# The second layer's scan: one 128-wide product for two heads, or one 64-wide product for each

## The chip, the cores and the metric

The kernel runs on one core of a Trainium2 chip. The metric is the device time of one execution in microseconds (us), as the median of three runs; a run without a profile and the profiled execution differ by well under a tenth of a per cent here.

## The reference

A decoder trunk of two residual layers over 512 tokens and a width of 2048, all in float32. The first is gated differential attention. The second, which the change is in, is RWKV-7 time mixing: `p = h @ w_in` gives r, k, v, a gate and two low-rank inputs, each mixed with the token before, and then every one of 32 heads of 64 channels runs a recurrence over the tokens with a 64 x 64 state S:

```
def step(S, inp):
    r_t, w_t, k_t, v_t, a_t, b_t = inp
    sa = einsum('bhvk,bhk->bhv', S, a_t)
    S = S * w_t[:, :, None, :] + sa[..., None] * b_t[:, :, None, :] + v_t[..., None] * k_t[:, :, None, :]
    y = einsum('bhvk,bhk->bhv', S, r_t)
    return S, y
```

with `a = -kk` and `b = kk * iclr` (kk is the normalised key). The y of a head is normalised, weighted, gated and projected: `x + (y * silu(g)) @ w_out`.

## The kernel before

The recurrence is not stepped token by token. Tokens are cut into 8 chunks of 64 (`NC_ = 8`, `C = 64`), and a chunk becomes a few small matrix products. Two heads are handled together as a pair (j = 0 to 15): head 0 lies on partitions 0 to 63 and head 1 on 64 to 127 (`HEADS`, slices `r_`).

`scan_pair` is the serial part. For each chunk c it makes three products that depend on one another, into one PSUM tile `sm`:

1. line 1558: `sm <- VS,G`. `VS[:, c]` holds, for each head, the state on the head's own 64 partitions and the chunk's values on the other 64. `G` holds the matching matrix, so state and values are summed over 128 partitions in one product.
2. line 1569: `sm <- rhs,TT`, the product with the triangular inverse of the chunk. `rhs` is product 1 copied out by ScalarE (line 1561, once for each head). `TT` is 128 x 128 with the two heads' 64 x 64 matrices on its diagonal and zeros beside them.
3. line 1576: `sm <- VS,BKT`, the state's increment. ScalarE has copied product 2 into `VS` (line 1571), and VectorE then decays and adds (line 1580, in chunk 0 line 1583) into the `VS` of the next chunk.

Of products 1 and 3 both heads are computed against both heads' columns, 128 x 128 outputs, of which the two diagonal blocks are read. GpSimd copies the states aside (`SA`, line 1564) and prepares the decayed state (`Sg`, line 1567). The last chunk has no product 3. In all there are 16 x 8 products 1, as many products 2, and 16 x 7 products 3: 368.

These chains run between the big projections. All weights are split into a high and a low part (`split_w`: ScalarE casts at line 105, VectorE subtracts at line 106), and `mm3` (line 124) makes three 512-wide products of each weight block. Every one of them calls `tick`, which counts down; when the gap that `scan_pair` has yielded is used up, the next step of the chain is issued right there in TensorE's program. So the three products of a step stand 4 to 8 big products apart. When a chain has done its chunks, `outputs` (lines 1598 and 1602) makes the reads of all chunks, in one burst: line 1598 takes a 128 x 64 stationary block and 64 columns, line 1602 a 64 x 64 block and 64 columns. `t_combine` (lines 1465 and 1476, 32 x 32 blocks) and `gram` (lines 1344 and 1361) make other small products, also in bursts.

In the profile a float32 product counts as two records of TensorE, each with its weight load (PEld); the big ones (float32r) count as one. "128*64" in a record is the part of the array it uses, rows by columns.

Of the kernel before, what the change touches and what calls it, by code (L numbers as in the profile page):

```python
# [23 lines left out]
P = 128  # L24
# [1167 lines left out]
C = 64  # L1192
# [342 lines left out]
HEADS = ((0, slice(0, C)), (1, slice(C, P)))  # L1535


def chain(g, j, p, delay, gap, gap_s, others=(), lead=GAP_D - GAP_T):
    def steps():
        yield from t_combine(g, j, p, lead)  # L1540
        yield from scan_pair(g, j, p, gap, gap_s, dict(others))

    p.chain = Chain(g, steps(), delay)
    return p.chain


def scan_pair(g, j, p, gap, gap_s, others):

    nc, w, VS = g.nc, g.work, p.VS
    both = lambda ap: ap.rearrange("p h n -> p (h n)")
    p.SA = w.tile([P, NC_ - 1, C], F32, name="SA", tag="SA", bufs=1)
    for h, r_ in HEADS:
        g.begun = nc.gpsimd.memset(VS[r_, 0, h, :], 0.0).ins
    for c in range(NC_):
        sm = g.ps.tile([P, 512], F32, name="sm", tag="pa", bufs=1)
        nc.tensor.matmul(sm[:, 0:P], both(p.G[:, c, 0]), both(VS[:, c]), start=True, stop=True)  # L1558
        rhs = w.tile([P, C], F32, name="rhs", tag="rhs", bufs=2)
        for h, r_ in HEADS:  # L1560
            nc.scalar.copy(rhs[r_, :], sm[r_, h * C : h * C + C])  # L1561
        if c:
            for h, r_ in HEADS:
                nc.gpsimd.tensor_copy(p.SA[r_, c - 1, :], VS[r_, c, h, :])  # L1564
        if 0 < c < NC_ - 1:
            Sg = w.tile([P, C], F32, name="Sg", tag="Sg", bufs=2)
            nc.gpsimd.tensor_scalar(Sg[:], p.SA[:, c - 1, :], p.gam[:, c : c + 1], None, ALU.mult)
        yield gap
        nc.tensor.matmul(sm[:, P : P + C], both(g.TT[j % 2][:, c]), rhs[:], start=True, stop=True)  # L1569
        for h, r_ in HEADS:  # L1570
            g.copied = nc.scalar.copy(VS[r_, c, h, :], sm[r_, P : P + C])  # L1571
        yield gap
        if c == NC_ - 1:
            break
        o = P + C
        nc.tensor.matmul(sm[:, o : o + P], p.BKT[:, c, :], both(VS[:, c]), start=True, stop=True)  # L1576
        for h, r_ in HEADS:
            s_ = sm[r_, o + h * C : o + h * C + C]
            if c:
                g.state = nc.vector.scalar_tensor_tensor(VS[r_, c + 1, h, :], s_, p.gam[r_, c : c + 1], Sg[r_, :],  # L1580
                                                         ALU.mult, ALU.add)
            else:
                nc.vector.tensor_scalar(VS[r_, c + 1, h, :], s_, p.gam[r_, c : c + 1], None, ALU.mult)
        if c in others:
            others[c]()
        yield gap_s
    outputs(g, j, p)
    centre(g, p)


def outputs(g, j, p):

    nc = g.nc
    p.Y = [g.ps.tile([P, 512], F32, name="Y", tag="pc", bufs=2) for _ in range(2)]
    place = lambda h, c: p.Y[h][c % 2 * C : c % 2 * C + C, c // 2 * C : c // 2 * C + C]
    for c in range(NC_):
        for h, _ in HEADS:
            nc.tensor.matmul(place(h, c), p.G[:, c, 1, h, :], p.VS[:, c, h, :], start=c < 2, stop=c == 0,  # L1598
                             skip_group_check=True)
    for c in range(1, NC_):  # L1600
        for h, r_ in HEADS:
            nc.tensor.matmul(place(h, c), p.AR[r_, c, 1, :], p.SA[r_, c - 1, :], start=False, stop=True,
                             skip_group_check=True)


def centre(g, p):

    nc, w, Y = g.nc, g.work, p.Y
    s1 = g.small.tile([P, NT, 2], F32, name="s1", tag="s1", bufs=3)
    p.yc = w.tile([P, 2 * NT, C], F32, name="yc", tag="yc", bufs=1)  # L1610
    for h in range(2):
        yg = Y[h][:, : NT * C].rearrange("p (t n) -> p t n", t=NT)
        nc.vector.reduce_sum(s1[:, :, h], yg, AX.X)
        nc.vector.tensor_scalar(s1[:, :, h], s1[:, :, h], 1.0 / C, None, ALU.mult)
        c = nc.vector.tensor_sub(p.yc[:, h::2, :], yg, s1[:, :, h : h + 1].to_broadcast([P, NT, C]))
    g.centred = c.ins
# [255 lines left out]
```

## Time and profile before

| | |
|---|---|
| median of 3 runs | 2055.09 us (2055.05 to 2055.22) |
| profiled execution | 2055.6 us, of which 2053.9 us from first to last instruction |
| TensorE (PE) busy | 2035.2 us, 99% |
| weight loads (PEld) busy | 1673.1 us, 81% |
| VectorE (DVE) busy | 1605.9 us, 78% |
| ScalarE (ACT) busy | 1133.6 us, 55% |
| GpSimd (POOL) busy | 400.3 us, 19% |
| clock granted to TensorE | 1.000 of full speed |

TensorE is busy nearly all the time, and the other engines run beside it. A row of the timeline reads: start, duration, engine, line, operation, output<-inputs, part of the array, shapes, count. The ends of matmuls are modelled and overlap the next one, so what a product takes of TensorE is read from starts: from the start of one to the start of the next. The scan of the 16 pairs lies between about 1008 and 1910 us.

### The profile page before, as it was taken

The numbers are of one execution on the slowest core, as the hardware profiler recorded it, in microseconds if no ns is written. First come the engines' busy times: TensorE is split into PE (matmuls) and PEld (weight loads), VectorE is DVE, ScalarE is ACT, GpSimd is POOL, SyncE is SP. The second block draws the span as 40 slices with busy tenths as digits, with TensorE's granted clock in tenths as the row PEclk, the third lists the DMA queues.
The fourth block names the chain that finished last, engine by engine and source line by source line (L and its number), as shares of the span: only waits on it lengthen the run. The fifth ranks groups of instructions, "written<-read, shape, count | busy, mean of one in ns | idle before, by whom it ended". The sixth has DMA issues, their size and how long they took to land.

```text
span 2053.9 us, 34174 instructions
## 1 busy us (share of the span) xinstructions
PE 2035.2 (99%) x11922; PEld 1673.1 (81%) x11922; DVE 1605.9 (78%) x4100; ACT 1133.6 (55%) x2258; POOL 400.3 (19%) x782
## 2 busy tenths in 40 slices
PE   9999999999999999999999999999999999999999
PEld 7888888888888888888877778888888888877887
DVE  7988988888898977476787888787777888777745
ACT  5765656666666544355565555555555555545423
POOL 1020111102011000121222222322222222231011
PEclk9999999999999999999999999999999999999999
DMA  8487978879787965823333323223333232346676
GB/s 288 156 163 192 182 172 186 164 192 167 190 180 171 274 218 172 175 87 108 103 83 92 94 77 98 92 89 98 98 98 98 87 96 83 111 127 201 212 182 145
DMA packets 159534, 297.76 MB, mean 145 GB/s; under 512 B 64529, under 2 KB 81937, under 8 KB 159361
## 3 DMA queue, kind: packets, MB, share of 16 engines
q1 hardware_dynamic: 110768, 184.39, 28.8%
q0 software_dynamic: 25952, 90.88, 23.2%
q10 hardware_dynamic: 22640, 20.30, 3.1%
q8 instruction: 94, 1.54, 0.3%
q14 instruction: 80, 0.65, 0.1%
HBM read 271.33 MB, written 24.18 MB: 144 GB/s over the span
## 4 chain that ended last, share of the span: by engine, by line
PE 90%; DVE 6%; ACT 2%; issue 1%; DMA 1%; SPq 0%; ACTq 0%; DVEq 0%
PE pp L124 45%; PE pp L574 24%; PE pt L124 5%; PE gp L1361 2%; DVE wl L106 2%; PE sm L1558 1%; PE sc L124 1%; PE o L124 1%; PE sm L1576 1%; PE sm L1569 1%; ACT wh L105 1%; PE Y L1598 1%; PE pt L296 1%; PE z L124 1%; PE pt L1393 1%
## 5 line engine op out<-in xcount | busy, mean ns | idle before, releaser
L106 DVE TENSOR_TENSOR wl<-wraw,wh 128x1024 fp32r<-128x1024 f32 (+1 forms) x286 | 349.7, 1223 | 167.7 <-ACT wh L105 157.0
L105 ACT CAST wh<-wraw 128x1024 fp32r<-128x1024 f32 (+1 forms) x286 | 299.5, 1047 | 237.6 <-PE pp L124 115.8
L124 PE MATMUL pp<-hL,wh 128*128 128x512 f32 x1024 | 413.6, 404 | 0.0
L124 PE MATMUL pp<-hH,wl 128*128 128x512 f32 x1024 | 413.0, 403 | 0.0
L124 PE MATMUL pp<-hH,wh 128*128 128x512 f32 x1024 | 412.3, 403 | 0.2 <-ACT wh L105 0.2
L124 PEld LDWEIGHTS pp<-hH,wh 128*128 128x128 f32 x1024 | 193.1, 189 | 34.5 <-ACT wh L105 0.4
L124 PEld LDWEIGHTS pp<-hL,wh 128*128 128x128 f32 x1024 | 193.1, 189 | 33.5
L124 PEld LDWEIGHTS pp<-hH,wl 128*128 128x128 f32 x1024 | 193.2, 189 | 32.4
L574 PE MATMUL pp<-wh,hH 128*128 128x512 f32 x448 | 176.8, 395 | 0.0
L574 PE MATMUL pp<-wh,hL 128*128 128x512 f32 x448 | 175.8, 392 | 0.0
L124 PE MATMUL pp<-wh,hH 128*128 128x512 f32 x376 | 147.0, 392 | 0.6 <-ACT hH L1147 0.6
L124 PE MATMUL pp<-wl,hH 128*128 128x512 f32 x376 | 147.5, 392 | 0.0
L124 PE MATMUL pp<-wh,hL 128*128 128x512 f32 x376 | 147.3, 392 | 0.1
L1420 DVE SCALAR_TENSOR_TENSOR tmpl<-LT,Tm 128x60 f32<-128x60 f32 (+24 forms) x496 | 134.8, 272 | 13.2
L574 PE MATMUL pp<-wl,hH 128*128 128x512 f32 x448 | 140.3, 392 | 0.0
L1564 POOL COPY SA<-VS 64x64 f32<-64x64 f32 x224 | 55.4, 248 | 397.8 <-DVE VS L1580 375.4
L1422 DVE TENSOR_TENSOR Tm<-Tm,tmpl 128x60 f32<-128x60 f32 (+24 forms) x496 | 103.4, 209 | 11.7
L1561 ACT COPY rhs<-sm 64x64 f32<-64x64 f32 x256 | 53.0, 207 | 84.8 <-PE sm L1558 81.8
L574 PEld LDWEIGHTS pp<-wl,hH 128*128 128x128 f32 x448 | 84.5, 189 | 17.2
L574 PEld LDWEIGHTS pp<-wh,hH 128*128 128x128 f32 x448 | 84.2, 188 | 17.5 <-issue 0.4
L574 PEld LDWEIGHTS pp<-wh,hL 128*128 128x128 f32 x448 | 84.3, 188 | 16.1
L1571 ACT COPY VS<-sm 64x64 f32<-64x64 f32 x256 | 52.9, 207 | 76.2 <-PE sm L1569 70.3
(435 smaller groups left out, 4374.4 us busy)
## 6 DMA issues: line engine op xcount, KB each, us to landing
wraw<-in_rw_w_in_dram SPq DMA_DIRECT2D x128, 512.0 KB
wraw<-in_da_w_in_dram SPq DMA_DIRECT2D x75, 512.0 KB
wraw<-in_da_w_in_dram POOLq DMA_DIRECT2D x28, 512.0 KB, 6.6
wraw<-in_da_w_out_dram SPq DMA_DIRECT2D x26, 512.0 KB
wraw<-in_rw_w_out_dram SPq DMA_DIRECT2D x24, 512.0 KB
Ta<-in_da_w_in_dram POOLq DMA_DIRECT2D x21, 512.0 KB, 5.6
Tb<-in_da_w_in_dram POOLq DMA_DIRECT2D x21, 512.0 KB, 5.7
Tc<-in_da_w_in_dram POOLq DMA_DIRECT2D x21, 512.0 KB, 5.5
```

Of the source, the lines that this page charges most:

```text
L105: a = nc.scalar.copy(hi[:, ks], raw[:, ks])
L106: d = nc.vector.tensor_sub(lo[:, ks], raw[:, ks], hi[:, ks].bitcast(F32))
L124: m = nc.tensor.matmul(out, a, b, start=s, stop=e, skip_group_check=skip)
L296: nc.tensor.transpose(pt[:, c * P : (c + 1) * P], t1s[t][:, c * P : (c + 1) * P], g.ident[:])
L574: m = nc.tensor.matmul(out[t][:], x, wt[lo][:, k, :], start=first, stop=end and lo == 1 and k == KG - 1, skip_group_check=True)
L1361: m = nc.tensor.matmul(gp[h][:, i * P : (i + 1) * P], BK[r_, c0 + i, :, :], p.AR[r_, c0 + i, :, :], start=True, stop=True)
L1393: nc.tensor.transpose(ps[:, i * P : (i + 1) * P], p.BK[:, c0 + i].rearrange("p s t -> p (s t)"), g.ident[:])
L1420: nc.vector.scalar_tensor_tensor(tt, LT[:, i : i + 1, i + 1 :].to_broadcast([P, s, n]), n2[:, i : i + 1], Tm[:, 0:s, i : i + 1].to_broadca ...
L1422: nc.vector.tensor_add(Tm[:, 0:s, i + 1 :], Tm[:, 0:s, i + 1 :], tt)
L1561: nc.scalar.copy(rhs[r_, :], sm[r_, h * C : h * C + C])
L1564: nc.gpsimd.tensor_copy(p.SA[r_, c - 1, :], VS[r_, c, h, :])
L1571: g.copied = nc.scalar.copy(VS[r_, c, h, :], sm[r_, P : P + C])
```

## The change

Each of the three products is issued once for each head, with the head's 64 output columns alone. Product 1 and 3 take 128 x 64 of stationary block and 64 moving columns for each head; product 2 takes the head's 64 x 64 block of `TT` and 64 columns. A head's result now lies on its own partitions, in the same 64 columns of `sm`, so `rhs` is filled by one copy of 128 partitions instead of two of 64. The copies into `VS` and the VectorE updates stay one for each head.

```
-        nc.tensor.matmul(sm[:, 0:P], both(p.G[:, c, 0]), both(VS[:, c]), start=True, stop=True)
+        for h, r_ in HEADS:
+            nc.tensor.matmul(sm[r_, 0:C], p.G[:, c, 0, h, :], VS[:, c, h, :], start=True, stop=True)
         rhs = w.tile([P, C], F32, name="rhs", tag="rhs", bufs=2)
-        for h, r_ in HEADS:
-            nc.scalar.copy(rhs[r_, :], sm[r_, h * C : h * C + C])
+        nc.scalar.copy(rhs[:], sm[:, 0:C])
...
         yield gap
-        nc.tensor.matmul(sm[:, P : P + C], both(g.TT[j % 2][:, c]), rhs[:], start=True, stop=True)
         for h, r_ in HEADS:
-            g.copied = nc.scalar.copy(VS[r_, c, h, :], sm[r_, P : P + C])
+            nc.tensor.matmul(sm[r_, C:P], g.TT[j % 2][r_, c, h, :], rhs[r_, :], start=True, stop=True)
+        for h, r_ in HEADS:
+            g.copied = nc.scalar.copy(VS[r_, c, h, :], sm[r_, C:P])
...
-        o = P + C
-        nc.tensor.matmul(sm[:, o : o + P], p.BKT[:, c, :], both(VS[:, c]), start=True, stop=True)
         for h, r_ in HEADS:
-            s_ = sm[r_, o + h * C : o + h * C + C]
+            nc.tensor.matmul(sm[r_, P : P + C], p.BKT[:, c, r_], VS[:, c, h, :], start=True, stop=True)
+        for h, r_ in HEADS:
+            s_ = sm[r_, P : P + C]
```

On TensorE, in the scan of a late pair, products 1 and 2 of a chunk (G and TT are the matrices of the chunk) stand so before:

```order
L124 MATMUL pp<-hL,wh 128x512
L1558 MATMUL sm<-VS,G_12808 128x128
L124 MATMUL pp<-hH,wl 128x512
L124 MATMUL pp<-hH,wh 128x512
L124 MATMUL pp<-hL,wh 128x512
L124 MATMUL pp<-hH,wl 128x512
L124 MATMUL pp<-hH,wh 128x512
L124 MATMUL pp<-hL,wh 128x512
L1569 MATMUL sm<-rhs,TT_9497 128x64
```

and after:

```order
L124 MATMUL pp<-hL,wh 128x512
L1558 MATMUL sm<-VS,G_12868 64x64 x2
L124 MATMUL pp<-hH,wl 128x512
L124 MATMUL pp<-hH,wh 128x512
L124 MATMUL pp<-hL,wh 128x512
L124 MATMUL pp<-hH,wl 128x512
L124 MATMUL pp<-hH,wh 128x512
L124 MATMUL pp<-hL,wh 128x512
L1569 MATMUL sm<-rhs,TT_9497 64x64 x2
```

The two heads' products stand side by side, the big products around them are where they were, and the gap is the same. So it is with nearly all of the 368. On ScalarE, in the same scan, the copies out of product 1 and what stands behind them were:

```order
L1394 COPY BKT<-pt 128x512
L1561 COPY rhs<-sm 64x64 x2
L105 CAST wh<-wraw 128x1024
L1187 ACTIVATE mixv<-pp,omu 128x512
L1571 COPY VS<-sm 64x64 x2
```

and are:

```order
L1394 COPY BKT<-pt 128x512
L1560 COPY rhs<-sm 128x64
L105 CAST wh<-wraw 128x1024
L1187 ACTIVATE mixv<-pp,omu 128x512
L1571 COPY VS<-sm 64x64 x2
```

One copy stands where two stood; here nothing else has moved.

More of the change, by code (lines that the diff above doesn't have):

```diff
@@ L1551, in scan_pair @@
     nc, w, VS = g.nc, g.work, p.VS
-    both = lambda ap: ap.rearrange("p h n -> p (h n)")
     p.SA = w.tile([P, NC_ - 1, C], F32, name="SA", tag="SA", bufs=1)
```

## The prediction

> **What bounds the kernel now.** I read the page's busy shares and the chain that ended last first, then the time by stage, then the groups of the three products, and last the timeline of single products, since the groups give durations and not what a product takes of TensorE.
>
> ```profile
> span 2053.9 us, 34174 instructions
> PE 2035.2 (99%) x11922; PEld 1673.1 (81%) x11922; DVE 1605.9 (78%) x4100; ACT 1133.6 (55%) x2258; POOL 400.3 (19%) x782
> PE 90%; DVE 6%; ACT 2%; issue 1%; DMA 1%; SPq 0%; ACTq 0%; DVEq 0%
> ```
>
> ```profile
> 1008.00:1910.00 902.00, 893.17 (x6463) 729.56 (x6462) 704.81 (x1955) 499.41 (x1160) 244.15 (x581) 1.00 0.35 102
> ```
>
> The second fence is the stage of the scan: its length, then busy time of PE, PEld, DVE, ACT and POOL, then the granted clock (1.00). TensorE stands idle 902.0 - 893.2 = 8.8 us of it. VectorE has 197 us to spare and ScalarE 403 us. So in this stage time is TensorE time: what a product takes there more or less shows in the end one for one, and what it saves on other engines shows only in those 8.8 us. The groups by shape (count, busy us, mean ns, idle of the engine before them):
>
> ```profile
> L1558 PE MATMUL sm<-VS,G 128*128 128x128 f32 x256 | 51.3, 281 | 3.3 <-DVE VS L1580 2.8
> L1576 PE MATMUL sm<-VS,BKT 128*128 128x128 f32 x224 | 43.9, 278 | 0.3
> L1569 PE MATMUL sm<-rhs,TT 128*128 128x64 f32 x256 | 43.6, 252 | 2.5 <-ACT rhs L1561 2.0
> ```
>
> Two records make a product, so these are 128, 112 and 128 products, 368 in all, and of the 8.8 us idle 3.3 + 0.3 + 2.5 = 6.1 us lie before them.
>
> **What a product takes before.** TensorE's timeline around each of the three, from the start of the big product ahead to the start of the second one behind:
>
> ```profile
> 1471.67 0.40 PE L124 MATMUL pp<-hH,wh 128*128 128x512 f32 x1
> 1471.91 0.38 PE L1558 MATMUL sm<-VS,G 128*128 128x128 f32 x2
> 1472.05 0.47 PE L124 MATMUL pp<-hL,wh 128*128 128x512 f32 x1
> 1472.36 0.39 PE L124 MATMUL pp<-hH,wl 128*128 128x512 f32 x1
> ...
> 1473.75 0.40 PE L124 MATMUL pp<-hH,wh 128*128 128x512 f32 x1
> 1473.98 0.33 PE L1569 MATMUL sm<-rhs,TT 128*128 128x64 f32 x2
> 1474.12 0.48 PE L124 MATMUL pp<-hL,wh 128*128 128x512 f32 x1
> 1474.44 0.39 PE L124 MATMUL pp<-hH,wl 128*128 128x512 f32 x1
> ```
>
> ```profile
> 1504.28 0.39 PE L124 MATMUL pp<-hL,wh 128*128 128x512 f32 x1
> 1504.51 0.38 PE L1576 MATMUL sm<-VS,BKT 128*128 128x128 f32 x2
> 1504.65 0.48 PE L124 MATMUL pp<-hH,wl 128*128 128x512 f32 x1
> 1504.96 0.40 PE L124 MATMUL pp<-hH,wh 128*128 128x512 f32 x1
> ```
>
> The spans are 1472.36 - 1471.67 = 0.69, 0.69 and 0.68 us. Two big products alone take 0.46 (next fence: 1627.00 to 1627.46). So each small product takes 0.23 us, 64 moving columns (L1569) no less than 128. The entry is free: the small product starts 0.24 us behind a big one, as a big one would.
>
> **What the new products take.** The same kernel already makes such products, in the burst of `outputs`: line 1598 uses 128*64 of the array with 64 columns, the shape of new products 1 and 3, and line 1602 uses 64*64, the shape of new product 2.
>
> ```profile
> 1627.00 0.40 PE L124 MATMUL pp<-hL,wh 128*128 128x512 f32 x1
> 1627.24 0.39 PE L124 MATMUL pp<-hH,wl 128*128 128x512 f32 x1
> 1627.46 0.40 PE L124 MATMUL pp<-hH,wh 128*128 128x512 f32 x1
> 1627.79 1.20 PE L1598 MATMUL Y<-VS,G 128*64 128x64 f32 x32
> 1628.92 0.68 PE L1602 MATMUL Y<-SA,AR 64*64 64x64 f32 x28
> 1629.53 0.50 PE L124 MATMUL pp<-hL,wh 128*128 128x512 f32 x1
> 1629.86 0.40 PE L124 MATMUL pp<-hH,wl 128*128 128x512 f32 x1
> ```
>
> Three things cost here that cost nothing above. Entry: the burst starts 1627.79 - 1627.46 = 0.33 us behind the big product, not 0.24. Exit: the big product behind it is followed by the next only after 1629.86 - 1629.53 = 0.33, because its weights were not loaded ahead. And there is a pause before that exit. For it, and for the passes within, cut the same timeline finer (short windows count the records begun so far):
>
> ```profile
> 1627.79 0.28 PE L1598 MATMUL Y<-VS,G 128*64 128x64 f32 x2
> ...
> 1627.79 0.34 PE L1598 MATMUL Y<-VS,G 128*64 128x64 f32 x4
> ```
>
> ```profile
> 1629.37 0.23 PE L1602 MATMUL Y<-SA,AR 64*64 64x64 f32 x2
> ```
>
> The first window ends at 1627.89 and holds two records, the second at 1627.91 and holds four. So two tiles of the array start side by side, and the second pass of both starts about 0.11 us after the first. The last pair of the burst starts at 1629.37, and the big product 1629.53 - 1629.37 = 0.16 us later, although a pass repeats about every 0.06 us. This is no matter of one burst. PEld's waits show all 16 entries, without a semaphore as cause, and a burst of another shape (32*32) does the same at both ends:
>
> ```profile
> PEld Y L1598 <- issue: 5.8, 16, 0.4
> ```
>
> ```profile
> 1008.58 0.39 PE L124 MATMUL pp<-hH,wl 128*128 128x512 f32 x1
> 1008.90 0.69 PE L1476 MATMUL px<-TT,X 32*32 32x32 f32 x32
> 1009.52 0.50 PE L124 MATMUL pp<-hH,wh 128*128 128x512 f32 x1
> 1009.86 0.40 PE L124 MATMUL pp<-hL,wh 128*128 128x512 f32 x1
> ```
>
> 5.8/16 = 0.36 us of waiting at each entry; 0.32 in and 0.34 out at the 32*32 burst. I read it as an array that must run empty whenever the division into tiles changes, and cannot load weights ahead across the change.
>
> **The sum.** A new product is two matmuls on two tiles, two passes each, with a big product ahead and behind in all but a few places. From the big one ahead to the second one behind: entry 0.33, first to second pass 0.11, second pass to the big product 0.16, that one to the next 0.33, together 0.93 us. Less the two big ones (0.46) it takes 0.47, where it took 0.23: 0.24 us more. 368 x 0.24 = 88.3 us. Each of the four readings is rounded to 0.01, so 0.22 to 0.26 us, 81 to 96 us in all.
>
> Where a transposition stands behind product 3 instead of a big product, it too is a 128*128 product whose weights come only after the exit, so I price those places alike.
>
> Taken back: the waits for operands. The 6.1 us idle before the three groups is a floor, for a late operand shows as idle only beyond the modelled tail of the product ahead. PEld's waits show more:
>
> ```profile
> PEld sm L1558 <- PE pp L124: 11.8, 23, 1.3
> PEld sm L1569 <- ACT rhs L1561: 8.4, 17, 1.4
> PEld sm L1576 <- ACT VS L1571: 5.4, 18, 0.5
> ```
>
> Those are 58 cases, 25.6 us in which some 0.2 of each lies under a running big product, leaving about 14. With the change each product gives the engines behind it 0.24 us more, and an operand up to 0.1 us late now hides under the emptying of the array. I take 8 us back, between 0 and 14.
>
> The copy of product 1 into `rhs`: one of 128 partitions instead of two of 64.
>
> ```profile
> L1561 ACT COPY rhs<-sm x256: 189/207/210, 1012.1 to 1905.0; 64x64 f32<-64x64 f32 x128
> L1580 DVEq EVENT_SEMAPHORE  x96: 21/21/21, 1018.7 to 1903.3; - x96
> ```
>
> 128 copies of 0.207 us go, 26.5 us of ScalarE, if the wider copy keeps that duration (same 64 elements on each partition; no row has this shape, so 0.1 to 0.4 us each). ScalarE has 403 us to spare, so it only shortens waits, in the 8 us already; were that room gone it would be worth up to the 26. VectorE's updates wait once for each head now, some 100 more waits at 0.021 us, 2 us in its 197 to spare; whoever waits for those updates (GpSimd's copies, and product 1 a gap later) starts no later. The matmuls with their semaphores in front wait for the same ones as before. No DMA, queue or big product is moved.
>
> So 2055.6 (profiled time) + 88.3 - 8 = 2135.9 us. The profiled execution is 0.5 above the median, so **2135 us**, 3.9% slower.
>
> **Rivals.** *Packing pays (faster).* If entry and exit cost nothing when only two small matmuls stand between big ones, what counts is the rate within the burst: 32 records from 1627.79 to 1628.92 are 0.035 us each, so four passes take 0.14 against 0.22 for two old passes. That is 0.08 x 368 = 29 us less, 2026 us. It decides as long as changing the tiles costs under 0.08 us a product; the rows above show 0.09 at the entry alone, at all 16 entries, so 4%. The Trainium skill, "TensorEngine Tiling (Array Packing)", section Theoretical Speedup, promises up to 2x where a dimension is 64 or less; by that, 0.23 would halve and the time would be 2055 - 42 = 2013 us. Its section Key Properties says that changing the tiling mode drains the engine, and there the trace agrees with the 0.36 us at each entry.
>
> *The heads run one after the other.* The matmuls of head 1 would start only when head 0's second pass has begun: one pass slot more, 1.13/16 = 0.07 us, 26 us in all, 2161 us. Against it stand the two and four records in the short windows; for it, that the burst's order of heads and tiles differs from the new one. 8%. The Trainium skill, "TensorE: Matmul & The Clock Gate", section The mechanism, says that matmuls start and end strictly in program order. By that rule head 1 would wait in just this way; the first two records of the burst, within 0.1 us, rather speak for both tiles starting at once.
>
> *Only the entry costs.* With four passes in flight the next big weights might load beside them, so that the exit is as cheap as today's: 0.10 us less, 37 us, 2098 us. The shortest burst in the trace has eight records:
>
> ```profile
> 1100.93 0.39 PE L124 MATMUL pp<-hH,wl 128*128 128x512 f32 x1
> 1101.25 0.42 PE L1344 MATMUL pt<-k,ones 128*32 128x128 f32 x8
> 1101.61 0.38 PE L1361 MATMUL gp<-AR,BK 64*128 64x128 f32 x2
> ```
>
> It pays 0.32 at its entry, and its successor waits until 0.36 after its first start; nothing shorter is shown. 10%.
>
> **Numbers.** My forecast 78%, the rivals 4, 8 and 10%. The range reaches from 2110, halfway to the cheap exit, to 2162, the serial heads; it covers the bounds of the forecast (81 less 14 up to 96: 2122 to 2151). About 0.2%, 4 us, is what a measurement can tell from no change. Faster 4%, slower 94%; the remaining 2% is for costs and savings that cancel.
>
> **What would show it.** In the changed profile a big product should start 0.33 us ahead of every scan product, 0.33 us should pass behind the first big one after it, PEld should show some 368 waits without a semaphore, and TensorE's part of the stage from 1008 us should grow to about 980 us. ScalarE should be 26 us less busy. The prediction is wrong if a scan product still follows a big one by 0.23 us, or if the stage grows by under 50 us.

## Result and the profile after

The changed kernel takes 2124.36 us (median of 5 runs, 2123.48 to 2126.27) against 2055.09 us (2053.97 to 2059.29): the ratio is 1.0335, 95% interval 1.032 to 1.035, 69 us slower. The forecast was 2135 us, 80 us slower, with a range of 2110 to 2162. The profiled execution took 2124.57 us, 69.0 more than the one before.

The page of the changed kernel, and its stage of the scan (length, then busy time of PE, PEld, DVE, ACT, POOL, then the clock):

```profile
span 2122.9 us, 35541 instructions
PE 2112.4 (100%) x12658; PEld 1640.8 (77%) x12658; DVE 1611.4 (76%) x4100; ACT 1101.8 (52%) x2130; POOL 398.3 (19%) x782
PE 93%; DVE 4%; ACT 1%; issue 0%; DMA 0%; ACTq 0%
```

```profile
1008.00:1985.00 977.00, 975.77 (x7225) 701.31 (x7223) 715.27 (x1970) 469.81 (x1034) 242.18 (x581) 1.00 0.32 96
```

TensorE has 736 more records and is busy 77 us longer, while PEld is busy 32 us less: the loads of 64 columns are shorter, so the time did not go into more loading. The idle time of TensorE in the scan fell from 8.8 to 977.0 - 975.8 = 1.2 us. This window holds 26 records more than the change adds, and 6 us less is left behind it than before (137.9 against 143.9), so for the same work the stage grew by about 69 us and not by 75. ScalarE is busy 32 us less.

TensorE's timeline around products 1 and 2, to be read as in the prediction:

```profile
1240.97 0.40 PE L124 MATMUL pp<-hL,wh 128*128 128x512 f32 x1
1241.30 0.34 PE L1558 MATMUL sm<-VS,G 128*64 128x64 f32 x4
1241.57 0.50 PE L124 MATMUL pp<-hH,wl 128*128 128x512 f32 x1
1241.90 0.39 PE L124 MATMUL pp<-hH,wh 128*128 128x512 f32 x1
...
1242.82 0.40 PE L124 MATMUL pp<-hL,wh 128*128 128x512 f32 x1
1243.15 0.33 PE L1569 MATMUL sm<-rhs,TT 64*64 64x64 f32 x4
1243.41 0.51 PE L124 MATMUL pp<-hH,wl 128*128 128x512 f32 x1
1243.75 0.40 PE L124 MATMUL pp<-hH,wh 128*128 128x512 f32 x1
```

Entry 0.33 us, exit 0.33 and 0.34, and 0.93 us from the first row to the fourth in both groups. That is 0.47 us for a small product, as forecast, against 0.23 before. In the short windows, the first up to 1241.40 and the second up to 1241.42:

```profile
1241.30 0.28 PE L1558 MATMUL sm<-VS,G 128*64 128x64 f32 x2
...
1241.30 0.34 PE L1558 MATMUL sm<-VS,G 128*64 128x64 f32 x4
```

Both heads start at once, and their second passes together 0.11 us later. PEld now waits at the scan products without a semaphore. Before, it did so at the bursts, and at line 1558 only 14 times (2.9 us):

```profile
PEld sm L1558 <- issue: 39.6, 110, 0.4
PEld sm L1569 <- issue: 32.7, 90, 0.4
PEld sm L1576 <- issue: 23.2, 67, 0.4
...
PEld Y L1598 <- issue: 5.7, 16, 0.4
```

That is 267 waits of 0.35 to 0.36 us each, of the 368 that were forecast. Most of the other products show a wait of the same length that the profile puts down to some engine, for instance 20 at line 1569 to a weight cast of ScalarE (7.3 us in all). And the groups of the three products have no idle time ahead of them any more:

```profile
L1558 PE MATMUL sm<-VS,G 128*64 128x64 f32 x512 | 43.0, 246 | 0.0
L1569 PE MATMUL sm<-rhs,TT 64*64 64x64 f32 x512 | 42.4, 242 | 0.0
L1576 PE MATMUL sm<-VS,BKT 128*64 128x64 f32 x448 | 37.6, 246 | 0.0
```

Their busy time is lower than before (123 us against 139), although each takes twice as much of TensorE. Busy counts a record from its start to its modelled end; the gap at the entry is covered by the modelled end of the big product ahead (0.40 us, though its successor starts after 0.33), and the uncovered load stands in the 0.50 us of the one behind. Whoever had compared these groups alone would have read a gain.

### The profile page after: what moved, and what is told of

The parts are those of the page before. It is cut to its first block, busy times and chain, and to the rows that moved or that the text cites. A ratio compares the mean times of both kernels' runs of the same rounds, so it can differ in the third digit from the quotient of the medians.

```text
span 2122.9 us, 35541 instructions
## 1 busy us (share of the span) xinstructions
PE 2112.4 (100%) x12658; PEld 1640.8 (77%) x12658; DVE 1611.4 (76%) x4100; ACT 1101.8 (52%) x2130; POOL 398.3 (19%) x782
## 4 chain that ended last, share of the span: by engine, by line
PE 93%; DVE 4%; ACT 1%; issue 0%; DMA 0%; ACTq 0%
PE pp L124 49%; PE pp L574 23%; PE pt L124 5%; PE sm L1558 2%; PE sm L1569 2%; PE gp L1361 1%; PE sc L124 1%; PE sm L1576 1%; PE o L124 1%; DVE wl L106 1%; PE Y L1598 1%; PE pt L1393 1%; ACT wh L105 1%; PE pt L296 1%; PE z L124 1%; PE lora L1104 1%
## 5 line engine op out<-in xcount | busy, mean ns | idle before, releaser
L124 PE MATMUL pp<-hH,wl 128*128 128x512 f32 x1024 | 417.4, 408 | 0.0
L1580 DVE SCALAR_TENSOR_TENSOR VS<-sm,gam,Sg 64x64 f32<-64x64 f32 x192 | 54.4, 283 | 60.1 <-PE sm L1576 38.3
```

The costliest lines, as they stand in the source:

```text
L124: m = nc.tensor.matmul(out, a, b, start=s, stop=e, skip_group_check=skip)
```

## Experiments

The theory: what costs is the change of the array's division between a big product and a scan product, paid once per visit (one stop at the small products between two big ones), in (0.10 us) and out (the pause and the uncovered load); the passes within are cheap. The rivals: the number of small matmuls costs; the heads run one after the other; and, for the 11 us by which the forecast was too high, that the single copy into `rhs` gave them.

### Each product alone

Edits: line 1558 with the copy of `rhs`, line 1569, or line 1576 as in the diff, the other two as before.

> Product 1 alone is made per head (rhs then takes one copy); products 2 and 3 stay as they were. Theory (each change of the tile division costs a fixed entry and exit, about 0.24 us more for a product than the 0.23 it took): 128 x 0.235 = 30 us more, less some 6 us of operand waits that the longer product hides: 2079 us, and only the 128 products at line 1558 lie 0.33 us behind the big product ahead. Rival (the single copy into rhs is what gave time back): the give-back is larger here than with product 2 or 3 alone, 2070 us or less.

> Product 2 alone is made per head, two 64 x 64 blocks; the zeros beside them are no longer read, and both copies into rhs stay. Theory (fixed entry and exit): 128 x 0.237 = 30 us more, less some 5 us of waits: 2080 us. Rival (a 64 x 64 block is cheaper in its own right, since it is a quarter of the array's work): well under that, 2065 us.

> Product 3 alone is made per head. Theory: 112 products; some 78 stand between big products (0.237 us each), 34 ahead of transpositions (about 0.19 us): 25 us more, less some 3 us of waits: 2077 us. The three parts then add up to about the whole change (24 + 25 + 22 = 71 us against 69). Rival (cost comes from the three products together, for instance from a scan that falls behind): the parts add up to much less than the whole.

Measured, against 2056.22 us in the same session: product 1 alone 2074.06 us (ratio 1.0087, 1.0072 to 1.0102), product 2 alone 2077.70 (1.0104, 1.0087 to 1.0121), product 3 alone 2072.94 (1.0082, 1.0067 to 1.0097). Each is slower, by 17.8, 21.5 and 16.7 us with some 3 us either way, so no part of the change pays. All three are 3 to 6 us less slow than expected, and they add up to 56 us, not 69. The sum alone would leave room for the rival that the three products cost more together than apart. The starts in the traces rule it out: a product that is changed alone takes the same 0.92 to 0.93 us from the big product ahead to the second one behind as in the whole change (medians between big products). By 128 x 0.233, 128 x 0.237 and some 25 us the products cost 30, 30 and 25 us, so each alone takes back 8 to 12 us, and the whole change about 16. So the parts do not add up because what is taken back does not: it is one stock of operand waits, and each part alone gets half of it or more. By the measure explained further down, the late starts of the scan products sum up to 11.9 us in the trace before, and to 4.5, 5.6 and 7.8 us with products 1, 2 and 3 changed alone. Product 2 alone also met something else: its trace has a wait of 2.0 us at line 1638 with a lowered clock behind it, told at the end, which cost that execution about 3 us. Whether the single copy gave anything can't be read from 12 against 8 us at this precision; the next run asks it directly.

### The copy split again

```
-        nc.scalar.copy(rhs[:], sm[:, 0:C])
+        for h, r_ in HEADS:
+            nc.scalar.copy(rhs[r_, :], sm[r_, 0:C])
```

> The changed kernel with the copy into rhs split again, one for each head, 128 copies more on ScalarE. Theory (the time given back came from operand waits that a longer product hides, not from the copy): ScalarE 26 us busier and the time the same, 2124 us within 3. Rival (the single copy gave the extra 8 us back that the prediction missed): 2131 us or more.

Measured: 2125.89 us (ratio to before 1.0342, 1.0326 to 1.0357), 1.5 us over the changed kernel, which is within what these runs can tell. One copy in the changed kernel, and two here, by group:

```profile
L1560 ACT COPY rhs<-sm 128x64 f32<-128x64 f32 x128 | 27.2, 212 | 124.2 <-PE sm L1558 123.3
```

```profile
L1561 ACT COPY rhs<-sm 64x64 f32<-64x64 f32 x256 | 53.0, 207 | 124.3 <-PE sm L1558 121.9
```

The wide copy lasts 212 ns, the narrow one 207, so 26 us of ScalarE hang on this edit, and next to nothing of the end.

### Twice the matmuls in one visit

In the changed kernel, for all three products: `for h, r_ in HEADS:` becomes `for h, r_ in HEADS * 2:` over the matmul.

> The changed kernel with each per-head matmul issued twice in the same place (head 0, head 1, head 0, head 1; the second writes the same result again): twice the matmuls, no more changes of the tile division. Theory (entry and exit are paid once per visit, a further pass on both tiles costs about 0.058 us): 2 passes x 0.058 x 368 = 43 us over the changed kernel, 2167 us. Rival (the cost goes with the number of small matmuls, 0.24 us for each further pair): 88 us over it, 2212 us.

Measured: 2171.07 us (ratio to before 1.0562, 1.0547 to 1.0576), 46.7 us over the changed kernel; 43 were expected of the theory and 88 of the rival. Some 41 us are the passes (368 x 0.11, by the rows below); the trace also has a wait of 3.7 us at line 1637 that the changed kernel has not (0.3 us there).

```profile
1251.91 0.39 PE L124 MATMUL pp<-hL,wh 128*128 128x512 f32 x1
1252.23 0.45 PE L1558 MATMUL sm<-VS,G 128*64 128x64 f32 x8
1252.62 0.50 PE L124 MATMUL pp<-hH,wl 128*128 128x512 f32 x1
1252.95 0.39 PE L124 MATMUL pp<-hH,wh 128*128 128x512 f32 x1
```

Eight records instead of four, and 1252.95 - 1251.91 = 1.04 us instead of 0.93: 0.11 us for a second pair of matmuls, while the first pair takes 0.47. Entry and exit are the same as with four. So three quarters of what a visit costs, 0.36 of 0.47 us, do not depend on how much is done in it.

### Both heads on one tile

Product 1 in the changed kernel writes both heads to partitions 0 to 63:

```
-            nc.tensor.matmul(sm[r_, 0:C], p.G[:, c, 0, h, :], VS[:, c, h, :], start=True, stop=True)
+            nc.tensor.matmul(sm[0:C, 3 * C + h * C : 4 * C + h * C], p.G[:, c, 0, h, :], VS[:, c, h, :], start=True, stop=True)
...
-        nc.scalar.copy(rhs[:], sm[:, 0:C])
+        for h, r_ in HEADS:
+            nc.scalar.copy(rhs[r_, :], sm[0:C, 3 * C + h * C : 4 * C + h * C])
```

> The changed kernel with product 1 of both heads on one tile of the array (both results on partitions 0 to 63, side by side; two copies into rhs move them to the heads' partitions); products 2 and 3 stay one tile for each head. Theory (the heads run side by side because they lie on two tiles; on one tile the four passes follow each other, 0.058 us each): 2 x 0.058 us more for 128 products, 15 us over the changed kernel with two copies (2126 us), 2141 us. Rival (the heads run one after the other in the changed kernel too, and the 0.47 us is mostly pass time): no change, 2126 us.

Measured: 2139.16 us (ratio to before 1.04, 1.0383 to 1.0417), 13.3 us over the kernel with two copies, where 15 were expected and the rival had none.

```profile
1511.05 0.39 PE L124 MATMUL pp<-hH,wh 128*128 128x512 f32 x1
1511.37 0.45 PE L1558 MATMUL sm<-VS,G 128*64 128x64 f32 x4
1511.74 0.50 PE L124 MATMUL pp<-hL,wh 128*128 128x512 f32 x1
1512.08 0.39 PE L124 MATMUL pp<-hH,wl 128*128 128x512 f32 x1
```

The visit takes 1.03 us instead of 0.93 with the same four records. So in the changed kernel the two heads do run side by side, and the concurrency that the change buys is real: it is worth 0.10 us a visit, and the visit costs more than that.

### As many matmuls, one tile

Products 1 and 3 for each head's 64 moving columns, with all 128 stationary columns:

```
-        nc.tensor.matmul(sm[:, 0:P], both(p.G[:, c, 0]), both(VS[:, c]), start=True, stop=True)
+        for h in range(2):
+            nc.tensor.matmul(sm[:, h * C : h * C + C], both(p.G[:, c, 0]), VS[:, c, h, :], start=True, stop=True)
...
-        nc.tensor.matmul(sm[:, o : o + P], p.BKT[:, c, :], both(VS[:, c]), start=True, stop=True)
+        for h in range(2):
+            nc.tensor.matmul(sm[:, o + h * C : o + h * C + C], p.BKT[:, c, :], VS[:, c, h, :], start=True, stop=True)
```

> Products 1 and 3 made per head by their 64 moving columns, but with all 128 stationary columns, so that the whole array stays one tile; product 2 as before. Theory (0.11 us for a pass on the whole array, bound by its weight load): 240 products x 0.22 us = 53 us more, less some 9 us of waits: 2099 us. Rival (a pass goes with its moving columns: four passes of 64 cost what two of 128 cost): no change, 2055 us.

Measured: 2100.00 us (ratio 1.0216, 1.0202 to 1.023), as the theory has it.

```profile
1490.65 0.40 PE L124 MATMUL pp<-hH,wh 128*128 128x512 f32 x1
1490.88 0.55 PE L1559 MATMUL sm<-VS,G 128*128 128x64 f32 x4
1491.25 0.48 PE L124 MATMUL pp<-hL,wh 128*128 128x512 f32 x1
1491.56 0.40 PE L124 MATMUL pp<-hH,wl 128*128 128x512 f32 x1
```

The entry is 0.23 us, as free as before, and the four rows span 0.91 us. So 0.45 us go into four passes of 0.11 us: half the moving columns save nothing on the whole array. A product per head costs about the same whether the array is divided (0.47) or not (0.45), for quite different reasons.

### The old products twice

In the kernel before, each of the three products in `for _ in range(2):`.

> The kernel before with each of the 368 products issued twice (128-wide, the second writes the same result again): as many passes as in the changed kernel, and no change of the tile division. Theory (a pass on the whole array is held up by its weight load, 0.11 us, whatever else; operand waits of some 11 us are hidden by any longer product): 368 x 0.22 = 81 us more, less 11: 2125 us, with no waits without a semaphore in front of the products. Rival (only the per-head form shortens the waits, by its single copy or its earlier results): 81 us more, less 3 at most: 2133 us.

Measured: 2150.81 us (ratio 1.0466, 1.0452 to 1.048), 95.6 us more; neither 2125 nor 2133 held. The passes cost what was expected, 368 x 0.22 = 81 us. But the operand waits did not shrink, they grew. The one for the update of `VS`, 2.8 us before, is now

```profile
PE sm L1559 <- DVE VS L1583: 13.4, 16, 1.1
```

In this kernel line 1583 is that update. It comes late in nearly every pair, between 1275 and 1863 us once in each and by about 1.0 us, for a reason that stands on VectorE:

```profile
1337.81 1.22 DVE L106 TENSOR_TENSOR wl<-wraw,wh 128x1024 fp32r<-128x1024 f32 x1
1338.94 0.28 DVE L1420 SCALAR_TENSOR_TENSOR tmpl<-LT,Tm 128x66 f32<-128x66 f32 x1
1339.26 0.75 DVE L1188 SCALAR_TENSOR_TENSOR mixk<-pp,mu,mixk 128x511 f32<-128x511 f32 x1
1339.92 0.22 DVE L1422 TENSOR_TENSOR Tm<-Tm,tmpl 128x66 f32<-128x66 f32 x1
1340.06 0.59 DVE L1583 SCALAR_TENSOR_TENSOR VS<-sm,gam,Sg 64x64 f32<-64x64 f32 x2
```

The update stands behind a weight split and a token mix in VectorE's order. Directly behind a token mix (line 1188) stand 11 pairs of updates in this trace, and none in the trace before. On TensorE it looks so:

```profile
1339.39 0.39 PE L124 MATMUL pp<-hH,wh 128*128 128x512 f32 x1
1340.79 0.68 PE L1559 MATMUL sm<-VS,G 128*128 128x128 f32 x4 [1.01 <-DVE VS L1583]
```

The next product 1 starts 1.40 us behind its predecessor instead of 0.23. So a longer product does not hide operand waits by itself. It does if the order on the other engines leaves the operand where it was. The expectation took that for granted.

### More distance between products

```
-((6, 8) if j > LAG + 1 else (5, 6)) if full else (4, 4) if j > LAG else (4, 5)
+((6, 8) if j > LAG + 1 else (5, 6)) if full else (5, 5) if j > LAG or j == 1 else (4, 5)
```

> The kernel before with five big products between the products of the scan instead of four, in the scans of pairs 0 and 14 only, where most of the operand waits lie (about 2.4 and 2.9 us of the 12). Theory (the waits are real TensorE time, and more distance hides them): 3 to 5 us faster, 2051 us. Rival (the scan then ends later and what hangs on it waits instead): no change or slower.

Measured: 2064.70 us (ratio 1.0047, 1.0033 to 1.006), 9.5 us slower: the rival. Waits of TensorE in this run:

```profile
PE sm L1558 <- DVE VS L1580: 4.0, 9, 0.9
PE px L1465 <- DVE T L1459: 3.3, 3, 2.1
PE pp L124 <- DVE wl L106: 2.0, 1, 2.0
```

The products at line 1558 wait no less (4.0 us against 2.8 before), and other work waits more: line 1465 3.3 us against 2.0, and a big product 2.0 us for its weights. Over the span TensorE is idle 23.6 us against 18.7. That is 5 of the 9.5 us; a lowered clock, told at the end, is about 1 more, and the rest is not placed. That the later end of the scan causes these waits fits the rival, but no run isolates it. No version came out of this that beats the kernel before, and none was found in the others.

## Why the prediction was right, point by point

- *TensorE bounds the scan, so its time shows one for one.* Right: 77 us more of TensorE's busy time against 69 us more in the end; the difference is idle time that went, over the span from 18.7 to 10.5 us. The stage did not grow to the 980 us that were named as a sign, but, for the same work, to about 971; the 977 above is a matter of where the window ends.
- *Entry, passes, exit: 0.93 us, thus 0.47 for a product.* Right to 0.01 us, for both shapes, from bursts of 28 and 32 records to visits of four. That the cost belongs to the visit and not to the matmuls is shown by the doubled matmuls (0.11 us for the second pair), and that it comes with the divided array is shown by as many products on the undivided one (entry 0.23 us). The rows show that no weights are loaded ahead across the change of division; that the array runs empty in between is a reading of them.
- *Both heads at once.* Right, shown by the single tile (13.3 us for 128 products, 0.10 us each). The strict order of matmuls that the Trainium skill states ("TensorE: Matmul & The Clock Gate", The mechanism) does not put head 1 behind head 0's second pass here, as the prediction had worked it out for that rival: in the short windows above two records have begun by 1241.40, and the second passes come 0.11 us later.
- *Packing pays.* Out. The passes are cheaper, as this rival has it: a second pair in the same visit costs 0.11 us, a second undivided product 0.22. But the change of the division, which had to stay under 0.08 us a product, costs 0.36 us a visit with entry and exit.
- *Exit as cheap as today.* This rival is out: 0.33 to 0.34 us after every visit between big products, four records or eight.
- *Product 3 ahead of transpositions priced alike.* Slightly off. At the 14 places ahead of line 1502 the starts in the timeline, less the two big products, give 0.69 us before and 0.86 after: 0.17 more, not 0.24; at the others about 0.20. On 34 products this is some 2 us. Ten more stood inside a run of transpositions at line 1393 before and stand behind it now; over the same records it is the usual 0.24 us there.
- *Taken back: 8 us, between 0 and 14.* This is the term that was mis-sized, bound included. With 0.235 us for most products and 0.17 to 0.20 at the 34, the gross cost is about 85 us, and 69 remained: about 16 us came back. The starts of the products say where from. Take each start less that of the record ahead, less the usual distance (0.234 us behind a big product, 0.11 behind a transposition, 0.093 more with the entry): where that leaves over 0.02 us, it sums up to 11.9 us in the trace before, and to 0.9 us after. A late product also delays the big one behind it, as here:

```profile
1500.89 0.39 PE L124 MATMUL pp<-hL,wh 128*128 128x512 f32 x1
1501.21 0.46 PE L1558 MATMUL sm<-VS,G 128*128 128x128 f32 x2
1501.43 0.48 PE L124 MATMUL pp<-hH,wl 128*128 128x512 f32 x1
```

The product starts 0.32 us behind the big one instead of 0.23, without a mark of idle time, and the next big one 0.22 us behind it instead of 0.14. Over the 45 late products between big ones in the trace before this second part comes to 4.0 us, and it is nothing after, where the distance is 0.26 us everywhere. Another 1.1 us came from line 1465, whose wait fell from 2.0 to 0.9 us. Together that is the 16 us. The prediction took too little because it left part of the waits in place and had no term for the second part; the entry and 0.24 us more distance took nearly all. That it depends on VectorE's order as well, the doubled old products show.

- *The copy of `rhs`, VectorE's extra waits: nothing.* Right within 1.5 us, and within VectorE's 715 us busy of 977. (ScalarE is 32 us less busy where 26 were forecast; the copies alone, 53.0 to 27.2 us, are 26.)
- *The range.* Its lower end, 2110, is called halfway to the cheap exit, but halfway between 2135 and 2098 is 2116. Nothing hangs on it: the result lies above both.

## What to carry to other kernels

Small matmuls on tiles of a divided array pay when many stand together; between products on the whole array each visit costs a fixed 0.36 us here, whatever is done in it, and 0.11 us for each pair. The undivided products take 0.23 us for the first and 0.22 for each further one. An estimate from these figures is that three pairs in one visit come out even (0.69 against 0.67 us) and four gain (0.80 against 0.89); no run here has tried it. So ask how many visits a change makes before counting passes. The price can be read before the change from any burst of that shape: from the start of the big product ahead to the start of the second behind it, never from the busy time of the groups, which here even fell. And time that a bounding engine gains or loses is partly met by operand waits, of which there is one stock: three edits that each win from it do not win three times.

## What the runs showed of the hardware that was not expected

A pass on the whole array cost 0.11 us with 64 moving columns as with 128 (0.45 us for four passes, 0.23 for two). So splitting the product by heads saves nothing as long as the array stays whole. On two tiles a pair of heads took 0.11 us where it was the second in its visit, half of the undivided product; it is the entry and exit that turn this into a loss.

A wait can cost more than its length. In the run with longer gaps TensorE waited 2.14 us once, and the big products behind it stood 0.43 us apart for some 2.5 us:

```profile
1172.34 0.96 PE L1465 MATMUL px<-T,G 32*32 32x32 f32 x30 [2.14 <-DVE T L1459]
1173.23 0.80 PE L124 MATMUL pp<-hH,wl 128*128 128x512 f32 x1
1173.83 0.63 PE L124 MATMUL pp<-hH,wh 128*128 128x512 f32 x1
1174.25 0.63 PE L124 MATMUL pp<-hL,wh 128*128 128x512 f32 x1
```

```profile
1173.30:1176.10 2.80, 2.80 (x8) 2.23 (x8) 1.05 (x1) 0.73 (x2) 2.74 (x4) 0.53 0.26 83
```

The second fence gives the granted clock of that stretch, 0.53 of full speed: about 0.2 us lost on each of some six products. In the trace before, a wait of 2.0 us at the same line had no such sequel, so it does not follow every wait of this length. In the kernel with product 2 alone it followed a wait of 2.0 us at line 1638, and lasted longer:

```profile
1892.00:1896.00 4.00, 4.00 (x10) 2.84 (x9) 2.05 (x4) 2.42 (x5) 0.55 (x1) 0.50 0.98 372
```

The big products there stand 0.43 us apart from 1892.3 to 1895.7. With what lies around them some 3 us were lost in that execution, about as much as that part of the change looked dearer than the others.
